# Ten modulation units summed on the tensor engine in four column groups, and one projection load issued earlier

## The chip, the cores and the metric

The kernel runs on one core of a Trainium2 chip. The metric is the device time of one execution in microseconds (us), the median of several. Matrix products run on the tensor engine (PE in the profile; PEld is its weight load, which overlaps), elementwise work on the vector engine (DVE) and the scalar engine (ACT); GpSimd (POOL) does little here, and the sync engine (SP) issues the DMA loads. Each engine works through its own queue in the order written there and waits at an instruction whose operands are not ready. Products accumulate in PSUM, in banks that hold 512 floats on each of 128 partitions.

## The reference

Two encoder layers over 256 tokens of width 1024: latent attention (MLA) and a dense feed-forward network (FFN) in layer 0, a Mamba-2 mixer and eight experts in layer 1. Each sublayer is modulated by shifts, scales and gates that come from a single conditioning row `c`:

```python
cond = jax.nn.silu(c)                                   # (1, 1024)
for i in range(DEPTH):
    mod = cond @ ada_w[i] + ada_b[i]                    # (1, 6144)
    sh1, sc1, g1, sh2, sc2, g2 = jnp.split(mod, 6, axis=-1)
    h = modulate(rmsnorm(x, norm_g[i, 0]), sh1, sc1)
    ...                                                 # y = mla_mixer(h, ...) or mamba2_mixer(h, ...)
    x = x + g1[:, None, :] * y
    h = modulate(rmsnorm(x, norm_g[i, 1]), sh2, sc2)
    ...                                                 # y = swiglu(h, ...) or moe_swiglu(h, ...)
    x = x + g2[:, None, :] * y
```

`cond @ ada_w[i]` is a product of one row with a 1024 x 6144 matrix, all float32: 4 MB of weights for every 1024 columns, and each weight is used once.

## The kernel before

The 6144 columns of a layer's `ada_w` are cut into 12 **units** of 512 columns. A unit is 1024 x 512 floats, loaded as two 1 MB tiles `raw` of 4 x 128 rows each (unit 2 as one of 4 and two of 2). Units 0 and 1 of layer 0 are the shifts `sh1` (channels 0 to 511 and 512 to 1023), 2 and 3 the scales `sc1`, 4 and 5 the gates `g1`, 6 and 7 `sh2`, 8 and 9 `sc2`. The result is wanted with channels on partitions, four columns of the tile `mod` for each unit.

A unit's product is made without the tensor engine's matrix work: row block k of the weights (128 rows) is multiplied by a scalar per partition, `cond[:, k]`, and added up over the eight blocks. This gives `acc`, 128 x 512, whose sum over partitions is still to be made. For units 4 to 9 that is one ACT instruction (`ada_sum`, L218) and seven on DVE (L220); for units 0 to 3, which stand at the start of the program, `ada_sums` makes two half sums per unit (L248 on ACT, L250 and L252 on DVE). Then matmuls with a column of ones (L229 in `ada_unit`, L263 in `ada_pair`), 128 columns of `acc` at a time, sum over partitions and put the result on partitions; a DVE addition of the bias (L231, L266) ends a unit. `ada_pair` also runs 34 matmuls on `ones` that nothing reads (`keep_warm`, L272).

The work around it, in the order of the program. `x` is loaded and transposed (L430). Units 0 and 2 give shift and scale of channels 0 to 511 (`make_gsc`, L280); `normmod` makes `tt` (L341, DVE) and `h` (L343, ACT) of these channels, blocks k = 0 to 3; the input projection, in plain float32, takes block after block (L448, six matmuls per block: `win_mm`), reading three loads of the projection's weights (`win`, blocks 0-2, 3-5 and 6-7). Units 1 and 3 do the same for blocks 4 to 7. Then come the norms of the latents (L303, L316, L317, L328), keys and values (L516, copied out by `v_sb` L548), and four rounds of queries (L516, L567, L573) and attention (scores `sc` L581 and L582, exponentials L588 and L590, transposes `tp` L597, outputs `o` L602 to L604); the rounds carry units 4 to 7, one each. The output projection (L358 to L360, on pairs of high and low parts) has two halves, which carry units 8 and 9. Its residual (L376) feeds the next norm (L303 to L328) and the FFN's first matmul (`gu`, L358).

A scheduler sets the order on each engine from the order of the code and its own costs, so rounds overlap: a unit's instructions are spread among those of the attention. SP's queue is the order of the loads. A tile `raw` is one of a pool of buffers; a load waits until its buffer's last reader is done.

The matmuls are float32 in two passes: one matmul leaves two records in the trace ("x96" are 48 matmuls).

Of the kernel before, what the change touches and what calls it, by code (L numbers as in the profile page):

```python
# [11 lines left out]
F32 = mybir.dt.float32  # L12
# [3 lines left out]
AF = mybir.ActivationFunctionType  # L16
ALU = mybir.AluOpType
AX = mybir.AxisListType
PSUM = bass.MemoryType.PSUM

P = 128
# [48 lines left out]
def rows(ap, n, off=0):  # L70

    return bass.AP(tensor=ap.tensor, offset=ap.offset + off, ap=[[P, n], [1, P]])
# [8 lines left out]
def body(ctx: ExitStack, tc, x, c, positions, ada_w, ada_b, norm_g,  # L81
# [5 lines left out]
    V, A, PE, G, SP = nc.vector, nc.scalar, nc.tensor, nc.gpsimd, nc.sync  # L87

    per = ctx.enter_context(tc.tile_pool(name="per", bufs=1, side="left"))
    rawp = ctx.enter_context(tc.tile_pool(name="rawp", bufs=8, side="left"))  # L90
    hlp = ctx.enter_context(tc.tile_pool(name="hlp", bufs=4, side="left"))
# [4 lines left out]
    nrm = dctx.enter_context(tc.tile_pool(name="nrm", bufs=2, side="right"))  # L96
# [11 lines left out]
    def pt(tag):  # L108
        pool, tag, n = banks[tag]
        return pool.tile([P, 512], F32, tag=tag, name=tag, bufs=n)  # L110
# [12 lines left out]
    def load(ap, k):  # L123

        n = ap.shape[1]
        t = raw(k * n).rearrange("p (k n) -> p k n", k=k)
        SP.dma_start(t, ap.rearrange("(k p) n -> p k n", p=P))
        return t
# [58 lines left out]
    cond = pd.tile([P, DC], F32, name="cond")  # L187
    A.activation(cond, cT, AF.Silu)
    ones = per.tile([P, P], F32, name="ones")
# [1 line left out]
    V.memset(ones, 1.0)  # L191
    eps_t = per.tile([P, 1], F32, name="eps_t")
    V.memset(eps_t, EPS)
    few = per.tile([P, 3], F32, name="few")
    warm, halfpi, zero = few[:, 0:1], few[:, 1:2], few[:, 2:3]
    V.memset(zero, 0.0)

    ej = per.tile([P, 2, S + 2 * NE], F32R, name="ej")
# [3 lines left out]
    ident = cst[:, C_ID:C_ID + P]  # L202
    vecs = pd.tile([P, 3, P], F32, name="vecs")

    vecT = pd.tile([P, 3, P], F32, name="vecT")
    mod = pd.tile([P, 2, 48], F32, name="mod")
# [6 lines left out]
    def ada_load(i, u):  # L213
        return load8(ada_w[i, :, u * 512:(u + 1) * 512])
# [7 lines left out]
    def ada_unit(i, u):  # L222

        acc = nrm.tile([P, 512], F32, tag="acc", name="acc")
        ada_sum(ada_load(i, u), acc)
        ps = pt("m")
        if i == 0 and u < 10:
            for m in range(4):
                PE.matmul(ps[:, m:m + 1], acc[:, m * P:(m + 1) * P], ones[:, 0:1], start=m == 0, stop=True,  # L229
                          skip_group_check=True)  # L230
            V.tensor_add(mod[:, i, 4 * u:4 * u + 4], ps[:, 0:4], vecT[:, 0, 48 * i + 4 * u:48 * i + 4 * u + 4])  # L231
        else:
            for m in range(4):
                PE.transpose(ps[:, m * P:(m + 1) * P], acc[:, m * P:(m + 1) * P], ident)
            dst = mod[:, i, 4 * u:4 * u + 4]
            for m in range(4):
                A.activation(acc[:, m * P:(m + 1) * P], ps[:, m * P:(m + 1) * P], AF.Copy,
                             accum_out=dst[:, m:m + 1])
            V.tensor_add(dst, dst, vecT[:, 0, 48 * i + 4 * u:48 * i + 4 * u + 4])

    def ada_sums(w):

        both = hlp.tile([P, 1024], F32, tag="wlo", name="acc2")
        acc = [both[:, z * 512:(z + 1) * 512] for z in range(2)]
        for k, wk in enumerate(t[:, k, :] for t in w for k in range(t.shape[1])):
            a = acc[k % 2]
            if k == 0:
                A.activation(a, wk, AF.Copy, scale=cond[:, k:k + 1])  # L248
            elif k == 1:
                V.tensor_scalar(a, wk, cond[:, k:k + 1], None, op0=ALU.mult)  # L250
            else:
                V.scalar_tensor_tensor(a, wk, cond[:, k:k + 1], a, op0=ALU.mult, op1=ALU.add)  # L252
        return acc

    def ada_pair(u, sums, warm=(0, 0)):

        ps = pt("m")
        for i, acc in enumerate(sums):
            keep_warm(warm[i])
            for z in range(2):  # L260
                for m in range(4):
                    c = 4 * i + m
                    PE.matmul(ps[:, c:c + 1], acc[z][:, m * P:(m + 1) * P], ones[:, 0:1],  # L263
                              start=z == 0 and c == 0, stop=z == 1, skip_group_check=True)
        four = lambda t: t.rearrange("p (i c) -> p i c", c=8)[:, :, 4 * u:4 * u + 4]
        V.tensor_add(four(mod[:, 0, 0:16]), ps[:, 0:8].rearrange("p (i c) -> p i c", c=4), four(vecT[:, 0, 0:16]))  # L266

    def keep_warm(n, bank="mm"):

        ps = pt(bank) if n else None  # L270
        for _ in range(n):
            PE.matmul(ps[:, :P], ones, ones, start=True, stop=True)  # L272

    gsc = pd.tile([P, 2, 2, DC], F32, name="gsc")

# [113 lines left out]
    with ExitStack() as lctx:  # L389
# [7 lines left out]
        def win_load(k0, n):  # L397
            return load(mla_w_in[0, k0 * P:(k0 + n) * P, :], n)


        SP.dma_start(cst[:, 0:C_V], consts[:, 0:C_V])
        x_in = load(x[0], 2)
        SP.dma_start(vecs[0:96, 0, :], rows(ada_b, 96))
        SP.dma_start(vecs[96:128, 0, :], rows(norm_g, 32))
        aw = {0: ada_load(0, 0)}
# [2 lines left out]
        SP.dma_start(vecs[0:3, 2, :], rows(mla_q_norm, 3))  # L408
        SP.dma_start(vecs[3:5, 2, :], rows(mla_kv_norm, 2))
        SP.dma_start(vecs[5:21, 2, :], rows(ssm_norm, 16))  # L410
        win = [win_load(0, 3)]
        aw[1] = ada_load(0, 1)
        aw[3] = ada_load(0, 3)
        pos_i = mi.tile([P, S], I32, tag="t2", name="pos_i", bufs=2)
        SP.dma_start(pos_i, bcast(positions, S))
        win += [win_load(3, 3), win_load(6, 2)]
        SP.dma_start(cst[:, C_V:], consts[:, C_V:C_KEY])


# [6 lines left out]
        for q in range(4):  # L426
            ps = pt("mm")
# [3 lines left out]
            A.copy(xT[:, 2 * q:2 * q + 2, :], ps.rearrange("p (a s) -> p a s", a=2))  # L431
        r = spread(pt("n"), r)
        vec_block(0, 128)
        sums = ada_sums(aw[0]), ada_sums(aw[2])
        ada_pair(0, sums, (8, 26))
        make_gsc(0, 0, 0, 4)
        normmod(0, 0, r, range(4), whole=h32)

# [10 lines left out]
                          skip_group_check=True)  # L449
        for k in range(4):  # L450
            win_mm(k, kv + rq + qq)
        sums = ada_sums(aw[1]), ada_sums(aw[3])
        ada_pair(1, sums)
        make_gsc(0, 0, 4, 8)
        normmod(0, 0, r, range(4, 8), whole=h32)

# [81 lines left out]
        wk = [packed(wkv[k][:, :, 0:64].unsqueeze(1)) for k in range(2)]  # L538
        for t in range(8):
            ps = pt("mm")  # L540
# [3 lines left out]
        for j in range(2):  # L544
            for nh in range(2):
                ps = pt("mm")
# [60 lines left out]
        for b in range(4):  # L607
            queries(b)
            attend(2 * b)
            attend(2 * b + 1)  # L610
            ada_unit(0, 4 + b)
        for half in range(2):
            w = load8(mla_w_out[0, :, half * 512:(half + 1) * 512])
            for m in range(2):
                ps = pt("mm")
                ws = unit8(w, m * 256, 256)
                for t in range(2):
                    mm3(ps[:, t * S:(t + 1) * S], list(zip(cols(ws, slice(t * P, (t + 1) * P)), at)))
                for t in range(2):
                    resid(ps[:, t * S:(t + 1) * S], 4 * half + 2 * m + t, 0, 0)  # L620
            ada_unit(0, 8 + half)
        make_gsc(0, 1)

    ph = scoped(dctx, "ph")
# [69 lines left out]
    with ExitStack() as lctx:  # L694
# [36 lines left out]
        ps, psb0 = pt("in"), pt("y")  # L731
# [9 lines left out]
        four = nrm.tile([P, 4, 2, SH], F32, tag="sq", name="four", bufs=2)  # L741
        xb, e, z, w = (four[:, i, :, :] for i in range(4))
        q = e
# [60 lines left out]
        m = decay_tiles()  # L804
# [808 lines left out]
```

## Time and profile before

| | |
|---|---|
| three runs | 1290.25, 1292.62, 1293.30 us (median 1292.62) |
| profiled execution | 1291.27 us, its span 1289.1 us |
| PE busy | 1244.1 us, 97% of the span |
| DVE busy | 857.4 us, 67% |
| ACT busy | 698.4 us, 54% |
| chain that ended last | PE 86%, DMA 4%, DVE 4%, ACT 3%, issue 2% |

The stage that the change touches, layer 0's attention with its modulation, is the first 162 us of the span; from the FFN on the program is as before. "Busy" counts a matmul until its modelled end, so PE at 97% is not PE at its peak: whether it streams or waits has to be read from the starts of its instructions. The chain of waits follows the last instruction back to what released it, piece by piece.

### The profile page before, as it was taken

What the parts mean: (1) busy time and instruction counts of PE and PEld (TensorE: products, weight loads), DVE (VectorE), ACT (ScalarE), POOL (GpSimd) and SP (SyncE); (2) the same over time, 40 slices, a digit from 0 to 9 for tenths busy, and PEclk for the clock granted to TensorE, in tenths of its full rate; (3) what the DMA queues carried; (4) which work ended last, traced back from release to release, by engine and by line L of the source; (5) the groups of instructions that cost most, each with busy time, mean ns of one, the idle gap of its engine ahead of it and who ended that gap; (6) DMA issues with size and microseconds to landing.
All of it is one profiled execution on the core that took longest, in us unless ns stands there. A gap on an engine that the chain in (4) does not pass through costs nothing.

```text
span 1289.1 us, 21161 instructions
## 1 busy us (share of the span) xinstructions
PE 1244.1 (97%) x8236; PEld 1006.7 (78%) x8236; DVE 857.4 (67%) x1314; ACT 698.4 (54%) x1162; POOL 18.3 (1%) x16
## 2 busy tenths in 40 slices
PE   7999999999999999998999999999999999999996
PEld 6768899999988999996648875488855688888652
DVE  7577787787789788853148870388902789988412
ACT  3468564455577767524157650477603676776312
POOL 4010000000000000000000000000000000000000
PEclk9999999999989999997999999999999999999999
DMA  9885569887933466425999999999999999998895
GB/s 343 313 299 188 196 239 349 325 308 272 321 124 127 164 213 213 164 99 203 421 422 419 421 394 409 421 421 420 395 382 420 420 421 398 387 352 312 329 421 214
DMA packets 104730, 407.96 MB, mean 316 GB/s; under 512 B 10401, under 2 KB 16046, under 8 KB 70958
## 3 DMA queue, kind: packets, MB, share of 16 engines
q1 hardware_dynamic: 104622, 406.53, 81.5%
q8 instruction: 66, 1.08, 0.3%
q14 instruction: 42, 0.34, 0.1%
HBM read 405.46 MB, written 1.05 MB: 315 GB/s over the span
## 4 chain that ended last, share of the span: by engine, by line
PE 86%; DMA 4%; DVE 4%; ACT 3%; issue 2%; SPq 0%; ACTq 0%; DVEq 0%
PE a L1291 18%; PE a L1383 12%; PE y L1336 10%; DMA raw<-in_moe_w_down_dram 4%; PE y L1402 3%; PE y L358 3%; PE gu L358 3%; PE gu L359 3%; PE gu L360 3%; PE y L359 3%; PE y L360 3%; PE in L360 2%; PE in L358 2%; PE in L359 2%; PE mm L448 2%
## 5 line engine op out<-in xcount | busy, mean ns | idle before, releaser
L159 DVE TENSOR_TENSOR wlo<-raw,whi 128x1024 fp32r<-128x1024 f32 x395 | 466.3, 1218 | 83.4 <-ACT whi L159 81.7
L159 ACT CAST whi<-raw 128x1024 fp32r<-128x1024 f32 x395 | 403.7, 1050 | 185.6 <-PE a L1291 41.6
L1383 PE MATMUL a<-raw,xe 128*64 128x384 f32 (+3 forms) x1280 | 161.6, 413 | 0.0
L1291 PE MATMUL a<-wlo,xe_hi 128*128 128x512 f32 (+1 forms) x464 | 153.2, 343 | 0.4
L1291 PE MATMUL a<-whi,xe_lo 128*128 128x512 f32 (+1 forms) x464 | 151.9, 339 | 0.0
L1383 PEld LDWEIGHTS a<-raw,xe 128*64 128x64 f32 x1280 | 92.0, 135 | 68.1 <-issue 51.7
L1304 DVE TENSOR_TENSOR sg<-sg,a 128x512 f32<-128x512 f32 (+2 forms) x36 | 22.0, 640 | 157.0 <-PE a L1383 145.1
L1291 PE MATMUL a<-whi,xe_hi 128*128 128x256 f32 (+1 forms) x464 | 111.2, 344 | 7.8 <-ACT whi L159 7.8
L220 DVE SCALAR_TENSOR_TENSOR acc<-raw,cond,acc 128x512 f32<-128x512 f32 x140 | 105.5, 766 | 5.8 <-ACT acc L218 4.3
L358 PE MATMUL gu<-hT_hi,whi 128*128 128x256 f32 x352 | 99.7, 284 | 1.2 <-ACT hT_hi L345 1.2
L1291 PEld LDWEIGHTS a<-wlo,xe_hi 128*128 128x128 f32 x464 | 87.0, 188 | 16.6 <-DVE wlo L159 4.2
L359 PE MATMUL gu<-hT_lo,whi 128*128 128x256 f32 x352 | 99.6, 283 | 0.0
L360 PE MATMUL gu<-hT_hi,wlo 128*128 128x256 f32 x352 | 99.1, 282 | 0.0
L1291 PEld LDWEIGHTS a<-whi,xe_lo 128*128 128x128 f32 x464 | 87.2, 188 | 9.7
L1291 PEld LDWEIGHTS a<-whi,xe_hi 128*128 128x128 f32 x464 | 75.9, 188 | 24.0 <-ACT whi L159 14.9
L1402 PE MATMUL y<-raw,at 128*64 128x512 f32 (+1 forms) x364 | 81.6, 586 | 0.9 <-DMA raw<-in_moe_w_down_dram 0.6
L358 PE MATMUL in<-hT_hi,whi 128*128 128x256 f32 (+1 forms) x264 | 75.9, 288 | 0.7 <-ACT whi L159 0.7
L360 PE MATMUL in<-hT_hi,wlo 128*128 128x256 f32 (+1 forms) x264 | 75.5, 287 | 0.5 <-DVE wlo L159 0.5
L359 PE MATMUL in<-hT_lo,whi 128*128 128x256 f32 (+1 forms) x264 | 74.7, 283 | 0.0
L358 PEld LDWEIGHTS gu<-hT_hi,whi 128*128 128x128 f32 x352 | 67.0, 191 | 1.5 <-ACT hT_hi L345 1.5
L360 PEld LDWEIGHTS gu<-hT_hi,wlo 128*128 128x128 f32 x352 | 67.0, 190 | 0.0
L359 PEld LDWEIGHTS gu<-hT_lo,whi 128*128 128x128 f32 x352 | 67.0, 190 | 0.0
(399 smaller groups left out, 2281.7 us busy)
## 6 DMA issues: line engine op xcount, KB each, us to landing
raw<-in_moe_w_gate_dram SPq DMA_DIRECT2D x88, 1024.0 KB, 7.1
raw<-in_moe_w_up_dram SPq DMA_DIRECT2D x88, 1024.0 KB, 12.8
raw<-in_moe_w_down_dram SPq DMA_DIRECT2D x85, 1024.0 KB, 15.9
raw<-in_ada_w_dram SPq DMA_DIRECT2D x47, 1024.0 KB, 8.0
raw<-in_ssm_w_in_dram SPq DMA_DIRECT2D x20, 1024.0 KB, 5.2
raw<-in_ffn_w_down_dram SPq DMA_DIRECT2D x11, 1024.0 KB, 8.4
raw<-in_ffn_w_gate_dram SPq DMA_DIRECT2D x10, 1024.0 KB, 8.4
raw<-in_ffn_w_up_dram SPq DMA_DIRECT2D x10, 1024.0 KB, 9.4
```

The lines of the kernel that those rows point to most:

```text
L159: return A.copy(hi, src), V.tensor_sub(lo, src, hi)
L220: V.scalar_tensor_tensor(acc, w[k // 4][:, k % 4, :], cond[:, k:k + 1], acc, op0=ALU.mult, op1=ALU.add)
L358: PE.matmul(ps, whi, ahi, start=(first and i == 0), stop=False, skip_group_check=skip)
L359: PE.matmul(ps, whi, alo, start=False, stop=False, skip_group_check=skip)
L360: PE.matmul(ps, wlo, ahi, start=False, stop=(last and i == n - 1), skip_group_check=skip)
L448: PE.matmul(ps, win[k // 3][:, k % 3, sl], h32[:, k, :], start=first and k == 0, stop=k == DC - 1, skip_group_check=True)
L1291: PE.matmul(bank[:, o:o + n], a[:, j, :], w[:, m], start=f, stop=l, skip_group_check=True)
L1304: V.tensor_mul(self.sg[:, sl], self.sg[:, sl], self.acc["u", b][:, :n])
L1336: PE.matmul(self.y[b], a, w[:, b * 512:(b + 1) * 512], start=f, stop=l, skip_group_check=True)
L1383: PE.matmul(bank[FEW * h:FEW * (h + 1), o // 2:(o + n) // 2], self.xhi[:, j, :], w[:, h, :], start=first, stop=last, skip_group_check=True)
L1402: res = PE.matmul(self.y[c0 // 512][FEW * h:FEW * (h + 1), c0 % 512:c0 % 512 + n], self.at[t][:, FEW * h:FEW * (h + 1)], ws[h], start=t == ...
```

## The change

Units 0 to 9 of layer 0 no longer go through DVE and ACT sums. `ada_rows` makes eight matmuls per unit: row block k of the weights is the moving operand (128 x 512), and the stationary operand is `cond[:, k]` repeated over 32 columns. Block k writes column group k mod 4, that is 32 of the bank's 128 partitions; blocks 4 to 7 accumulate onto blocks 0 to 3. DVE copies the bank to SBUF (`row`), and `ada_columns` makes four 128 x 1 matmuls per unit against `one4`, a column that is 1 on one partition of each group and 0 elsewhere: this adds up the four groups and puts the result on partitions. `keep_warm` is gone. Units 10 and 11 of layer 0 and all of layer 1 stay as they were.

The second load of the projection's weights (blocks 3 to 5) moves ahead of units 1 and 3, the third ahead of `pos_i`, and unit 3 is loaded in pieces of 4, 2 and 2 row blocks.

```diff
+    def ada_rows(w):
+
+
+        ps = pt("mm")
         for k, wk in enumerate(t[:, k, :] for t in w for k in range(t.shape[1])):
...
+            g = k % 4 * 32
+            PE.matmul(ps[g:g + 32, :], cond[:, k:k + 1].to_broadcast([P, 32]), wk, start=k < 4, stop=k >= 4,
+                      skip_group_check=True)
+        row = nrm.tile([P, 512], F32, tag="acc", name="row")
+        V.tensor_copy(row, ps)
+        return row
+
+    def ada_columns(units, rows):
 
         ps = pt("m")
...
+        for i, (u, row) in enumerate(zip(units, rows)):
+            for m in range(4):
+                PE.matmul(ps[:, 4 * i + m:4 * i + m + 1], row[:, m * P:(m + 1) * P], one4, start=i == m == 0,
+                          stop=True, skip_group_check=True)
+        for i, u in enumerate(units):
+            V.tensor_add(mod[:, 0, 4 * u:4 * u + 4], ps[:, 4 * i:4 * i + 4], vecT[:, 0, 4 * u:4 * u + 4])
...
+        V.reduce_sum(one4, ident.rearrange("p (g q) -> p g q", g=4)[:, :, 0], axis=AX.X)
...
-        win = [win_load(0, 3)]
+        win = [win_load(0, 3), win_load(3, 3)]
         aw[1] = ada_load(0, 1)
-        aw[3] = ada_load(0, 3)
+        u3 = ada_w[0, :, 1536:2048]
+        aw[3] = [load(u3[0:512, :], 4), load(u3[512:768, :], 2), load(u3[768:1024, :], 2)]
+        win += [win_load(6, 2)]
...
-        win += [win_load(3, 3), win_load(6, 2)]
...
-        sums = ada_sums(aw[0]), ada_sums(aw[2])
-        ada_pair(0, sums, (8, 26))
+        ada_columns((0, 2), [ada_rows(aw[u]) for u in (0, 2)])
...
-        sums = ada_sums(aw[1]), ada_sums(aw[3])
-        ada_pair(1, sums)
+        ada_columns((1, 3), [ada_rows(aw[u]) for u in (1, 3)])
...
-            ada_unit(0, 4 + b)
+            ada_columns((4 + b,), [ada_rows(ada_load(0, 4 + b))])
...
-            ada_unit(0, 8 + half)
+            ada_columns((8 + half,), [ada_rows(ada_load(0, 8 + half))])
```

In the changed kernel the new lines are L247 (the matmuls on the weights), L250 (the copy `row`), L258 (the column matmuls) and L261 (the addition); the lines behind them have numbers lower by 11 (L448 is L438 there, L358 is L347).

How the tensor engine's queue changes is shown at three places. First, the middle of the input projection: `mm` and `m` are PSUM tiles, `h32` the modulated input, a `raw` number is one loaded tile. Before, block 3 (raw_142, the second projection load) stood behind the column sums of units 1 and 3:

```order
L448 MATMUL mm_269<-h32_111,raw_130 128x256 x2
L263 MATMUL m_312<-ones_80,acc2_294 128x1 x8
L263 MATMUL m_312<-ones_80,acc2_303 128x1 x8
L448 MATMUL mm_267<-h32_111,raw_142 128x256 x2
L448 MATMUL mm_268<-h32_111,raw_142 128x256
```

The same place in the changed kernel (raw_133 is the second projection load, raw_135 to raw_143 are the pieces of units 1 and 3):

```order
L438 MATMUL mm_233<-h32_111,raw_133 128x256 x2
L247 MATMUL mm_258<-raw_135,cond_78 32x512 x4
L247 MATMUL mm_258<-raw_137,cond_78 32x512 x4
L247 MATMUL mm_269<-raw_139,cond_78 32x512 x4
L258 MATMUL m_280<-few_85,row_267 128x1 x4
L247 MATMUL mm_269<-raw_141,cond_78 32x512 x2
L247 MATMUL mm_269<-raw_143,cond_78 32x512 x2
L258 MATMUL m_280<-few_85,row_278 128x1 x4
L438 MATMUL mm_231<-h32_111,raw_133 128x256 x4
```

Block 3 now stands ahead of the units' matmuls, and nothing of the projection stands between these and block 4.

Second, the attention: unit 5's matmuls in the changed kernel (raw_770 and raw_772 are its two tiles; L591 to L593 are the attention's outputs, L570 and L571 its scores, L505 the next round's queries), with no counterpart before, where the tensor engine had only four column sums of unit 5:

```order
L247 MATMUL mm_774<-raw_770,cond_78 32x512
L591 MATMUL o_573<-pT_613,v_sb_416 64x128
L592 MATMUL o_573<-pT_613,v_sb_416 64x128
L593 MATMUL o_573<-pT_613,v_sb_416 64x128
L570 MATMUL sc_677<-kT_322,qT_321 128x128
L571 MATMUL sc_677<-kT_322,qT_321 128x256
L570 MATMUL sc_699<-kT_322,qT_321 128x128
L571 MATMUL sc_699<-kT_322,qT_321 128x256
L247 MATMUL mm_774<-raw_770,cond_78 32x512 x3
L247 MATMUL mm_774<-raw_772,cond_78 32x512 x4
L505 MATMUL mm_797<-lat0_399,wcp_793 128x256
```

The first of the eight stands alone, seven follow later. Unit 7's stand in three pieces (1, 4 and 3), unit 4's in two (5 and 3); units 6, 8 and 9 have their eight together.

Third, the end of the stage, before (L360 is the output projection, L303 the norm that follows):

```order
L359 MATMUL mm_1326<-aT_lo_529,whi_1331 128x256
L360 MATMUL mm_1326<-aT_hi_528,wlo_1332 128x256
L229 MATMUL m_1398<-ones_80,acc_1385 128x1 x4
L303 MATMUL m_1420<-ones_80,ss_1421 128x1 x2
L303 MATMUL m_1420<-ones_80,sq_1433 128x1 x2
```

and in the changed kernel:

```order
L348 MATMUL mm_1297<-aT_lo_490,whi_1302 128x256
L349 MATMUL mm_1297<-aT_hi_489,wlo_1303 128x256
L247 MATMUL mm_1360<-raw_1356,cond_78 32x512 x4
L247 MATMUL mm_1360<-raw_1358,cond_78 32x512 x4
L258 MATMUL m_1371<-few_85,row_1369 128x1 x4
L292 MATMUL m_1393<-ones_80,ss_1394 128x1 x2
L292 MATMUL m_1393<-ones_80,sq_1406 128x1 x2
```

Unit 9's matmuls, and its column sums that need the copy `row` of them, now stand between the last matmul of the output projection and the norm.

## Rows read from the trace of the kernel before

**Rows 1.** Windows: stretch and length, busy us (records) per engine, PE clock, DMA share, GB/s.

```profile
26.00:36.00 10.00, 10.00 (x35) 6.30 (x36) 9.85 (x16) 2.54 (x5) 0.00 (x0) 0.83 1.05 391
...
40.00:50.00 10.00, 10.00 (x40) 7.37 (x41) 5.26 (x17) 6.82 (x12) 0.00 (x0) 0.83 1.02 379
...
70.00:80.00 10.00, 8.96 (x37) 5.91 (x36) 6.20 (x11) 3.19 (x8) 0.00 (x0) 1.00 1.02 376
80.00:90.00 10.00, 8.96 (x40) 7.35 (x40) 7.10 (x17) 6.58 (x18) 0.00 (x0) 0.83 1.05 386
...
100.00:110.00 10.00, 9.76 (x64) 8.29 (x63) 8.63 (x28) 9.28 (x29) 0.00 (x0) 1.00 0.48 161
110.00:120.00 10.00, 10.00 (x67) 8.26 (x65) 7.40 (x23) 8.59 (x26) 0.00 (x0) 1.00 0.41 156
...
130.00:140.00 10.00, 8.41 (x60) 6.61 (x59) 8.91 (x21) 3.52 (x10) 0.00 (x0) 1.00 0.59 187
```

**Rows 2.** The chain of waits, first 60 us: start us, us, what.

```profile
19.00 0.81 DVE acc L252 x2
...
22.44 1.96 PE m L263 x16
...
24.43 0.17 DVE mod L266
...
25.95 10.57 PE mm L448 x36
36.53 3.47 PE m L263 x32
39.99 9.35 PE mm L448 x34
```

**Rows 3.** Timeline of ACT around 30 us: start, us, instruction, idle time before it.

```profile
30.40 0.72 ACT L248 ACTIVATE acc<-raw,cond 128x512 f32<-128x512 f32 x1 [2.43 <-DMA raw<-in_ada_w_dram]
```

**Rows 4.** Timeline of PE in the experts, near 643 us.

```profile
643.25 1.94 PE L1402 MATMUL y<-raw,at 128*64 128x512 f32 x8
645.12 0.39 PE L1200 MATMUL a<-psel,xt_lo 128*128 128x256 f32 x1
```

**Rows 5.** Groups of instructions by line, 60 to 157 us.

```profile
L220 DVE SCALAR_TENSOR_TENSOR acc<-raw,cond,acc 128x512 f32<-128x512 f32 x40 | 31.7, 810 | 0.4
L516 PE MATMUL mm<-lat,wcp 128*128 128x256 f32 x103 | 26.3, 403 | 0.8 <-DVE v_sb L548 0.8
...
L359 PE MATMUL mm<-aT_lo,whi 128*128 128x256 f32 x64 | 18.6, 293 | 0.0
...
L582 PE MATMUL sc<-kT,qT 98*128 98x256 f32 x32 | 9.7, 384 | 0.0
L597 PE MATMUL tp<-cst,pe 128*128 128x128 f32 x48 | 9.2, 278 | 0.0
...
L516 PE MATMUL mm<-raw,lat 128*128 128x512 f32 x16 | 7.0, 592 | 0.0
L602 PE MATMUL o<-pT,v_sb 128*64 128x128 f32 x32 | 6.9, 298 | 0.9 <-ACT pT L599 0.8
...
L581 PE MATMUL sc<-kT,qT 98*128 98x128 f32 x32 | 6.6, 288 | 1.0 <-ACT pe L590 1.0
...
L229 PE MATMUL m<-ones,acc 128*128 128x1 f32 x48 | 5.8, 242 | 0.3 <-DVE mod L231 0.3
...
L548 DVE COPY v_sb<-mm 128x512 f32<-128x512 f32 x4 | 2.7, 684 | 0.0
```

**Rows 6.** The chain of waits, 60 to 165 us.

```profile
97.12 0.36 PE o L602 x2
97.48 0.22 PE o L603 x2
...
114.45 0.43 PE mm L516 x2
...
122.17 0.12 PE mm L360
```

More of the change, by code (lines that the diff above doesn't have):

```diff
@@ L193, in body @@
     V.memset(eps_t, EPS)
-    few = per.tile([P, 3], F32, name="few")
-    warm, halfpi, zero = few[:, 0:1], few[:, 1:2], few[:, 2:3]
+    few = per.tile([P, 4], F32, name="few")
+    warm, halfpi, zero, one4 = (few[:, i:i + 1] for i in range(4))
     V.memset(zero, 0.0)
@@ L239, in ada_unit @@
             V.tensor_add(dst, dst, vecT[:, 0, 48 * i + 4 * u:48 * i + 4 * u + 4])
-    def ada_sums(w):
-        both = hlp.tile([P, 1024], F32, tag="wlo", name="acc2")
-        acc = [both[:, z * 512:(z + 1) * 512] for z in range(2)]
+    def ada_rows(w):
+        ps = pt("mm")
         for k, wk in enumerate(t[:, k, :] for t in w for k in range(t.shape[1])):
[L246 to L255, printed above, removed]
-        ps = pt("m")
[L258 to L272, printed above, removed]
+            g = k % 4 * 32
[5 more added lines that the diff above has]
+    def ada_columns(units, rows):
+        ps = pt("m")
+        for i, (u, row) in enumerate(zip(units, rows)):
[4 more added lines that the diff above has]
+            V.tensor_add(mod[:, 0, 4 * u:4 * u + 4], ps[:, 4 * i:4 * i + 4], vecT[:, 0, 4 * u:4 * u + 4])
     gsc = pd.tile([P, 2, 2, DC], F32, name="gsc")
```

## The prediction

> **What bounds the kernel now.** I read the windows first. In the attention stage the tensor engine is the busy one: from 60 to 157 us its windows are full but for four, which leave 1.04, 1.04, 0.24 and 1.59 us idle, 3.9 us together (one full window stands for the others) [rows 1]. [...] DVE is never full there, though it carries 40 sums of units 4 to 9, 31.7 us [rows 5].
>
> Busy is not streaming, so I counted the work from the steps between starts on the chain: 0.43 us for two records of 128x256, 0.22 for two of 128x128, 0.12 for one of L358 to L360 [rows 6]. Times the counts [rows 5] (L358 and L360 have as many records as L359, L603 and L604 as many as L602): queries and keys 103 x 0.215 = 22.1; output projection 192 x 0.12 = 23.0; values 7.0; scores 6.9 + 3.5; transposes 5.3; attention outputs 96 x 0.11 = 10.6; column sums about 5; norms and rotations about 2: 85 us of 97. The 12 us beside it are the 3.9 idle, the 1.7 of clock, up to 32 x 0.14 = 4.5 at the first of each output group (L602 0.36 against L603 0.22 [rows 6]), and 1.9 that I can't place. So whatever the sums on DVE hold up there is worth at most 12 us, and what is added to the tensor engine there is paid.
>
> The first 60 us are different. There the chain goes through the sums (19.00), the column sums (22.44), the addition (24.43) and the first projection matmuls (25.95), and again through the column sums at 36.53 to block 3 at 39.99 [rows 2]; the loads run at 391 GB/s without a pause, 1 MB in 2.7 us [rows 1].
>
> **The price of a unit on the tensor engine.** No row shows four groups at once. The nearest has two: four matmuls of 128x512, two in each group of 64 columns, start at 643.25 and let the next one start at 645.12, 1.87 us [rows 4]. One by one, at 7.0 us for 16 records [rows 5], they would take 3.5. So two groups run side by side in full: four rounds of 0.43, and 0.15 for the change of shape. With four groups side by side a unit's 16 records are four rounds, 1.72 + 0.15 = 1.87 us; with only two, 3.6; with none, 7.0. I take 1.87, since the row has all of its gain, and keep 3.6 for the range.
>
> [...]
>
> **First stage, units 0 to 3 and the moved load.** The sums of units 0 and 2 and `keep_warm` go. After 19.00 there remain two matmuls of unit 2's last piece (1.0), the copy `row` (0.68, as L548 [rows 5]), four column matmuls (8 records of 0.12, as 1.96 for 16 [rows 2]: 1.0), the same 1.52 from the addition to the first projection matmul (25.95 - 24.43), and hand-overs: 23.3 instead of 25.95, **-2.6**.
>
> Then 24 matmuls follow instead of 18, since block 3 is there early. 18 took 10.57 us for 7.7 us of work, because the clock was low in part (0.83 [rows 1, 2]). With the same loss of 2.9 they end at 23.3 + 10.3 + 2.9 = 36.5. The moved load puts units 1 and 3 back by 2.7 us: the first half of unit 3, waited for until 30.40 [rows 3], lands at 33.1 and its last piece near 35.8. That costs nothing, because these matmuls are behind block 3 in the queue anyway; without this cover it would be 2.7. From 36.5: units 1 and 3 and the first columns 4.9, the copy 0.7, columns 1.0, then 1.52 and hand-overs: block 4 starts at 44.8. Before, it starts at 39.99 plus six matmuls (2.6) plus the loss of a low clock (1.7, window 40 to 50): 44.3. So the first gain is given back: the columns and the modulation now stand between the last block of the first half and block 4, with nothing of the projection beside them, where before block 3 covered them. **+0.5**. From below: no clock lost ahead of block 4, -2.4. From above: that pause leaves the clock low for block 4, 1.7 more, +2.2.
>
> **Attention, units 4 to 9.** 40 sums on DVE and five on ACT go, six copies of 0.68 come. The column sums remain. Added are 48 matmuls on the weights. Units 6, 8 and 9 stand whole, 1.87 each. Pieces can't be packed: unit 4 in 5 and 3 costs 1.0 + 0.86 + 1.0, unit 5 in 1 and 7 costs 1.0 + 1.87, both 2.9; unit 7 in 1, 4 and 3 costs 3.0. **+14.4** of tensor work in a stretch that is full; 11.2 if the pieces stand in waits.
>
> Back come the waits that end with the sums. By name they are 0.8 on `v_sb` and 0.3 on the addition (sums ahead of both on DVE), 1.0 ahead of the first scores [rows 5], and with an engine that is never short of work the 1.7 of clock. The rest of the idle time is behind ACT's work on `aT` and `pT`, which remains but gets a freer queue. I take the idle time and clock in full, 5.6, and half of the unplaced 1.9: **-6.5**. Bounds: 3.8 and 12.
>
> **The end.** Unit 9's eight matmuls, the copy and the columns now stand between the output projection and the norm. Before, the sums were done by then. The copy is a wait that nothing behind it in the queue can fill: 0.68 and two hand-overs, **+0.9**; 0 if it hides behind the residual, 1.9 if it queues behind two residuals on DVE. The norm and the FFN are behind it, and from there the order is as before, so the delay is kept to the end.
>
> **Sum**: 0.5 + 14.4 - 6.5 + 0.9 = +9.3 on the profiled 1291.3 us gives 1300.6. The median of the runs lies 1.35 above that execution, 1301.9 by it; I say 1301.
>
> **Rivals.**
> 1. *Only two groups side by side.* 3.6 instead of 1.87 for a unit: about 9 more in the attention and 3.4 in the first stage, 1301 + 12 = 1313. For it: nothing shows four. Against: two cost nothing extra.
> 2. *The other side: the tensor engine waits more than its idle time says.* If all 12 us beside the counted work, the 4.5 at L602 too, are waits for `pT` and `pe` behind the sums on DVE and ACT, and the single pieces and the changes of shape stand in such waits (6 x 1.72 = 10.3): -2.4 + 10.3 - 12 + 0 = -4.1, 1287 on the profiled execution's scale and 1288.5 on the median's. It decides, for faster by more than 4 us, where the waits closed reach 11.9. For it: DVE at 8.9 of 10 in 130 to 140, the emptiest window of the tensor engine [rows 1]. Against: most windows are full.
> 3. *No change.* The early start is kept (-2.4), the pieces cost nothing (11.2), the waits return 7.5, the end costs 0.9: +2.2, 1294.
> 4. *The first stage's work doesn't count*, because loads set its end: then that term is 0, and the sum stays within a microsecond of mine; no case of its own.
>
> **Chances.** My forecast 0.42, between 1297 and 1306; two groups 0.15; no change 0.23; faster 0.2. About 0.3%, 4 us, is what a measurement tells from nothing. Faster by more 0.2, within 0.23, slower 0.57. The range for 8 in 10 runs from 1288, inside the second rival, to 1312, just short of the first.
>
> **What would show it.** In the changed profile: L247 of units 6, 8 and 9 at about 1.9 us for 16 records, with starts four at a time (3.6 and two at a time: first rival). The first projection matmul near 23.3, block 4 near 44.8. Full windows of the tensor engine from 60 on, a granted clock of 1.00 in 80 to 90, and DVE down by about 28 us; the FFN's first matmul about 9 us later than before. I am wrong if it comes no later, and then the term of the waits is the one that failed; if it comes on time with L247 as priced, there was more waiting among full windows than I counted.

## The result, and the profile after

The changed kernel takes 1305.76 us, the median of four runs (1302.77 to 1308.71), against 1292.59 of before in the same comparison: 1.0106 times, with a 95% interval of 1.0088 to 1.0124. It is slower by 13 us; the forecast was slower by 8, at 1301.

The page of the changed kernel's profile, its span and tensor engine, and the engines' shares of the chain that ended last:

```profile
span 1306.0 us, 21207 instructions
...
PE 1257.7 (96%) x8296; PEld 999.5 (77%) x8296; DVE 818.1 (63%) x1257; ACT 691.7 (53%) x1152; POOL 16.9 (1%) x16
...
PE 87%; DMA 4%; ACT 4%; DVE 3%; issue 1%; SPq 0%; DVEq 0%; ACTq 0%
```

The profiled execution took 1307.8 us, 2 more than the median, as that of before lies 1.3 below its own: the two traces differ by 16.9 us of span where the medians differ by 13. All of it has come up when the FFN begins: its first matmul starts at 179.24 instead of 162.15, 17.1 later. DVE has 39 us less to do (the forecast of 28 counted units 4 to 9 alone), and the kernel is slower all the same.

The windows that answer to [rows 1], of the changed kernel (stretch and length, busy us and records of PE, PEld, DVE, ACT, POOL, granted clock, DMA share, GB/s):

```profile
40.00:50.00 10.00, 7.51 (x41) 5.06 (x34) 6.32 (x19) 1.81 (x4) 0.00 (x0) 0.83 0.98 369
...
60.00:70.00 10.00, 10.00 (x48) 8.09 (x47) 3.54 (x9) 5.68 (x16) 3.92 (x4) 0.83 0.74 263
70.00:80.00 10.00, 10.00 (x32) 5.79 (x31) 2.77 (x4) 3.75 (x10) 0.00 (x0) 1.00 0.39 111
80.00:90.00 10.00, 9.32 (x46) 5.47 (x45) 3.21 (x8) 7.63 (x20) 0.00 (x0) 1.00 1.00 363
...
130.00:140.00 10.00, 10.00 (x73) 6.78 (x71) 6.09 (x19) 5.29 (x20) 0.00 (x0) 1.00 0.89 302
...
172.00:183.00 11.00, 9.27 (x45) 8.88 (x45) 4.77 (x14) 3.53 (x9) 0.00 (x0) 0.53 0.39 146
```

Most of the idle time has gone, as forecast: 70 to 80 and 130 to 140 are full where they had 1.04 us idle (waits for `v_sb` and an addition, both on DVE) and 1.59 (waits for `aT_hi` and `pT`, both from ACT). The low clock of 80 to 90 is gone, but 60 to 70 now has one, in a full window. New are also an idle quarter in 40 to 50, where before there was none, and a low clock for the whole end of the stage (0.53 in 172 to 183).

The chain of waits of the changed kernel in the first 50 us (start us, us, what):

```profile
21.74 0.24 DVE mod L261 x2
...
23.28 14.78 PE mm L438 x48
38.06 2.71 PE mm L247 x24
40.77 1.01 PE m L258 x8
...
42.87 0.70 DVE row L250
...
43.62 1.06 PE m L258 x8
...
46.31 9.84 PE mm L438 x36
```

Read against [rows 2]: the first projection matmul starts at 23.28, forecast 23.3. The 48 records of blocks 0 to 3 take 14.78 us for 10.3 of work. From 38 to 46 the chain goes through units 1 and 3, a copy, columns and the modulation, one after the other, and block 4 starts at 46.31, forecast 44.8 and 44.44 before.

The chain of the same kernel behind that, at the units and at the end of the stage:

```profile
100.35 0.98 PE mm L247 x2
...
116.69 1.85 PE mm L247 x16
...
129.66 0.97 PE mm L247 x2
...
131.72 0.99 PE mm L247 x8
...
134.22 0.99 PE mm L247 x6
...
167.56 0.42 DVE wlo L159
...
168.71 0.87 DVE xT L365 x2
169.58 1.13 DVE wlo L159
170.71 0.61 DVE row L250
...
171.37 1.05 PE m L258 x8
172.42 3.88 PE m L292 x20
...
179.24 0.80 PE gu L347 x2
```

A whole unit takes 1.85 us for 16 records (116.69), one matmul alone 0.97 or 0.98, a piece of 4 or 3 takes 0.99: the prices of the forecast to a few hundredths. So four column groups do run side by side: 16 records of 128x512 on all 128 columns took 7.0 us [rows 5], 16 in two groups 3.58 (the run with two groups). At the end unit 9's copy `row` stands on DVE behind a residual and behind a low part `wlo` of the FFN's first weights.

### The profile page after: what moved, and what is told of

Same layout as the page of the kernel before. It is cut to its first block, busy times and chain, and to the rows that moved or that the text cites. A ratio compares the mean times of both kernels' runs of the same rounds, so it can differ in the third digit from the quotient of the medians.

```text
span 1306.0 us, 21207 instructions
## 1 busy us (share of the span) xinstructions
PE 1257.7 (96%) x8296; PEld 999.5 (77%) x8296; DVE 818.1 (63%) x1257; ACT 691.7 (53%) x1152; POOL 16.9 (1%) x16
## 4 chain that ended last, share of the span: by engine, by line
PE 87%; DMA 4%; ACT 4%; DVE 3%; issue 1%; SPq 0%; DVEq 0%; ACTq 0%
PE a L1280 18%; PE a L1372 11%; PE y L1325 9%; PE y L1391 4%; PE y L347 3%; PE y L349 3%; PE y L348 3%; PE gu L347 3%; PE gu L348 3%; PE gu L349 3%; PE mm L505 2%; PE in L349 2%; PE in L347 2%; PE mm L438 2%; DMA raw<-in_moe_w_down_dram 2%; PE in L348 2%
## 5 line engine op out<-in xcount | busy, mean ns | idle before, releaser
L347 PE MATMUL gu<-hT_hi,whi 128*128 128x256 f32 x352 | 99.3, 283 | 1.2 <-ACT hT_hi L334 1.2
L349 PE MATMUL gu<-hT_hi,wlo 128*128 128x256 f32 x352 | 98.7, 280 | 0.0
L1280 PEld LDWEIGHTS a<-whi,xe_hi 128*128 128x128 f32 x464 | 76.0, 188 | 24.0 <-ACT whi L159 14.9
L347 PE MATMUL in<-hT_hi,whi 128*128 128x256 f32 (+1 forms) x264 | 76.0, 288 | 0.7 <-DVE r L303 0.7
L220 DVE SCALAR_TENSOR_TENSOR acc<-raw,cond,acc 128x512 f32<-128x512 f32 x98 | 72.3, 749 | 2.4 <-ACT acc L218 1.2
L347 PEld LDWEIGHTS gu<-hT_hi,whi 128*128 128x128 f32 x352 | 66.7, 190 | 1.5 <-ACT hT_hi L334 1.5
```

The source lines that it names most:

```text
L220: V.scalar_tensor_tensor(acc, w[k // 4][:, k % 4, :], cond[:, k:k + 1], acc, op0=ALU.mult, op1=ALU.add)
L347: PE.matmul(ps, whi, ahi, start=(first and i == 0), stop=False, skip_group_check=skip)
L349: PE.matmul(ps, wlo, ahi, start=False, stop=(last and i == n - 1), skip_group_check=skip)
L1280: PE.matmul(bank[:, o:o + n], a[:, j, :], w[:, m], start=f, stop=l, skip_group_check=True)
```

## The experiments

All of them are this kernel with the edit shown. The table gives the median, the ratio to the kernel before with its interval, and from each profile the start of the first projection matmul, of block 4, of the first transpose, of the output projection's last matmul, and of the FFN's first (us).

| kernel | median | ratio | first | block 4 | transposes | last out | FFN |
|---|---|---|---|---|---|---|---|
| before | 1292.6 | | 25.95 | 44.44 | 90.82 | 155.78 | 162.15 |
| changed | 1305.8 | 1.0106 [1.0088, 1.0124] | 23.28 | 46.31 | 92.43 | 167.64 | 179.24 |
| units 0-3 only | 1293.8 | 1.0028 [1.0008, 1.0049] | 23.42 | 46.18 | 93.81 | 160.13 | 166.14 |
| units 4-9 only | 1302.3 | 1.0086 [1.0065, 1.0106] | 25.76 | 45.28 | 88.03 | 163.22 | 175.24 |
| unit 9 on DVE | 1301.6 | 1.0086 [1.0066, 1.0105] | 23.23 | 44.96 | 90.90 | 166.11 | 173.72 |
| loads as before | 1303.0 | 1.0081 [1.0060, 1.0103] | 23.13 | 44.41 | 88.74 | 163.94 | 175.49 |
| two groups | 1324.1 | 1.0251 [1.0227, 1.0275] | 25.75 | 49.88 | 95.28 | 183.73 | 194.53 |
| units 8, 9 early | 1303.5 | 1.0097 [1.0074, 1.0120] | 23.38 | 46.22 | 92.27 | 169.82 | 177.08 |
| filler | 1306.8 | 1.0118 [1.0094, 1.0142] | 27.88 | 48.66 | 94.90 | 170.07 | 181.58 |
| units 0-3, loads as before, filler | 1293.6 | 1.0017 [1.0002, 1.0033] | 27.66 | 46.08 | 92.10 | 157.04 | 163.56 |
| units 0-3, loads as before | 1290.6 | 0.9992 [0.9976, 1.0009] | 23.08 | 44.61 | 89.64 | 154.79 | 160.96 |
| unit 4 only | 1298.0 | 1.0065 [1.0045, 1.0085] | 26.34 | 44.82 | 87.57 | 159.84 | 168.28 |
| units 0-4, loads as before | 1298.7 | 1.0058 [1.0038, 1.0079] | 23.17 | 43.17 | 87.50 | 159.76 | 167.70 |
| unit 4 only, early | 1294.7 | 1.0032 [1.0017, 1.0048] | 26.40 | 44.88 | 90.91 | 158.06 | 166.91 |

The medians of before in the shared comparisons were 1290.7 to 1292.0. The ratio and its interval are those of each comparison; the quotient of two medians can differ from it by a tenth of a per cent (units 0-3 only: 1.0014 by the medians). The intervals of "unit 9 on DVE", "loads as before" and "units 8, 9 early" overlap that of the changed kernel, so what these three bring is read from the starts in the table more than from the runs.

**Which part costs.** First the two halves of the change, each alone. Units 4 to 9 back on DVE:

```diff
-            ada_columns((4 + b,), [ada_rows(ada_load(0, 4 + b))])
+            ada_unit(0, 4 + b)
...
-            ada_columns((8 + half,), [ada_rows(ada_load(0, 8 + half))])
+            ada_unit(0, 8 + half)
```

> The changed kernel with units 4 to 9 summed on DVE again; units 0 to 3 and the loads stay as changed. Theory of the attention and the tail (the matmuls on the weights fill a tensor engine that was full from 90 us on, and unit 9's copy stands in the way of the norm): most of the 13 us goes, about 1296 remains, because block 4 of the projection still starts 2 us late and the clock is low twice behind it; the FFN's first matmul near 166. Rival, the first stage (its delay is carried through and is most of the loss, the attention's matmuls stand in waits): 1302 to 1305.

And the kernel before with only these two lines changed the other way (and the new helpers added):

> The kernel before with only units 4 to 9 moved to the tensor engine; units 0 to 3, the matmuls that nothing reads and the loads as before. Theory of the attention and the tail: 1301 to 1304, nearly all of the loss; 16 records of a unit take 1.85 us as in the changed kernel, and the last 12 us up to the FFN look as there. Rival, the first stage: within 3 us of before, 1290 to 1296.

1293.8 and 1302.3. The two delays at the FFN, 4.0 and 13.1 us, add up to the whole 17.1; by the ratios, 0.28% and 0.86% against 1.06%, whose intervals allow the same. The attention and the end are three quarters of the loss; that the first stage carried most of it is out.

**Is added tensor work paid?** Two groups of 64 columns instead of four of 32, the same matmuls:

```diff
-            g = k % 4 * 32
-            PE.matmul(ps[g:g + 32, :], cond[:, k:k + 1].to_broadcast([P, 32]), wk, start=k < 4, stop=k >= 4,
+            g = k % 2 * 64
+            PE.matmul(ps[g:g + 64, :], cond[:, k:k + 1].to_broadcast([P, 64]), wk, start=k < 2, stop=k >= 6,
...
-        V.reduce_sum(one4, ident.rearrange("p (g q) -> p g q", g=4)[:, :, 0], axis=AX.X)
+        V.reduce_sum(one4, ident.rearrange("p (g q) -> p g q", g=2)[:, :, 0], axis=AX.X)
```

> The changed kernel with two column groups of 64 instead of four of 32, the same matmuls in the same order, so only the price of a unit changes. Theory (the tensor engine is full from 90 us on, so its added work is paid): a unit of 16 records takes 3.6 us instead of 1.85, and with units 5 to 9 in the full stretch and the end the time rises by 8 to 12 us over the changed kernel, to 1314 to 1318. Rival (the matmuls on the weights stand in waits and the loss is elsewhere): up to 3 us more, 1306 to 1309.

1324.1, 18 us above the changed kernel and more than either side expected (its profile is 15.3 behind at the FFN): I had counted only units 5 to 9, and block 4 already starts 3.6 us later. The groups of this kernel by line, 60 to 190 us, and one whole unit on its chain:

```profile
L247 PE MATMUL mm<-raw,cond 128*64 128x512 f32 x96 | 26.6, 603 | 0.0
```

```profile
168.06 3.58 PE mm L247 x16
```

The changed kernel has 14.9 us in the group's place. Of the difference of 11.7, unit 9 has 1.7; the other 10.0 stand between the last input projection matmul and the output projection's end, and there this kernel needs 119.8 us (63.93 to 183.73) instead of 107.0 (60.65 to 167.64). What is added in the attention is paid, here with a surcharge of 2.8 that I can't place.

**The end of the stage.** From the output projection's last matmul to the FFN's first the changed kernel needs 11.6 us, the one before 6.4. Unit 9 alone back on DVE:

```diff
+            if half == 0:
+                ada_columns((8,), [ada_rows(ada_load(0, 8))])
+            else:
+                ada_unit(0, 9)
```

> The changed kernel with unit 9 alone summed on DVE again. In the changed kernel 11.4 us pass from the output projection's last matmul to the FFN's first, before 6.1. Theory: 1.9 us of unit 9's matmuls, 1.7 of waiting for its copy behind a weight's low part on DVE and the longer norm go, 4 to 5 us, so 1301. Rival (the sum on DVE comes late there and the tail waits as long, or the delay is one of the clock alone): within 2 us of the changed kernel, 1304 to 1307.

1301.6, 4 us less, and 7.6 us in that place instead of 11.6. Then everything kept on the tensor engine, but the matmuls and copies of units 8 and 9 written ahead of their half of the output projection:

```diff
             w = load8(mla_w_out[0, :, half * 512:(half + 1) * 512])
+            late = [ada_rows(ada_load(0, 8 + half))]
...
-            ada_columns((8 + half,), [ada_rows(ada_load(0, 8 + half))])
+            ada_columns((8 + half,), late)
```

> The changed kernel with the matmuls and the copy of units 8 and 9 written ahead of their half of the output projection instead of behind it; the column sums stay behind. Nothing is left out, the tensor engine's work is the same. Theory (behind the last half it is the wait for the copy and the stopped engine that cost, beside 1.9 us of matmuls that are paid either way): 2 to 4 us less than the changed kernel, 1302 to 1304. Rival (the tail costs only the matmuls): no difference, 1305 to 1307.

1303.5, 2 us less, and 2.2 at the FFN. Its timeline at the end of the stage shows the column sums right behind the projection, without the wait of 1.6 us:

```profile
169.82 0.28 PE L349 MATMUL mm<-aT_hi,wlo 128*128 128x256 f32 x1
169.93 0.95 PE L258 MATMUL m<-few,row 128*128 128x1 f32 x8
170.74 0.58 PE L292 MATMUL m<-ones,ss 128*128 128x1 f32 x4
```

The place needs 7.3 us; the output projection ends 2.2 later, for the matmuls that are now in front. So the end cost about 5 us: 1.9 of matmuls, and 3 of a copy behind DVE's queue and of the norm behind it.

**The moved load.** The loads in the order of before (and unit 3 in two pieces again), units on the tensor engine:

```diff
-        win = [win_load(0, 3), win_load(3, 3)]
+        win = [win_load(0, 3)]
         aw[1] = ada_load(0, 1)
...
+        aw[3] = ada_load(0, 3)
...
+        win += [win_load(3, 3), win_load(6, 2)]
```

> The changed kernel with the loads in the order of before: second and third projection load behind units 1 and 3, unit 3 in two pieces. Then units 1 and 3 land 2.7 us earlier, their matmuls stand ahead of block 3 in the tensor engine's queue, and block 3 covers columns, copy and modulation. Theory (the moved load takes that cover away): block 4 starts near 39 instead of 46.3, and 5 to 7 us go, 1299 to 1301. Rival (the second projection load then ends the stage, or the gain is lost to the clock): within 2 us of the changed kernel.

1303.0, 3 us less where 5 to 7 were expected. The timeline of its tensor engine, 22 to 47 us:

```profile
23.13 11.85 PE L437 MATMUL mm<-h,raw 128*128 128x256 f32 x36 [1.41 <-ACT h L332]
34.91 2.78 PE L247 MATMUL mm<-raw,cond 128*32 128x512 f32 x24
37.65 1.05 PE L258 MATMUL m<-few,row 128*128 128x1 f32 x8
38.63 1.06 PE L247 MATMUL mm<-raw,cond 128*32 128x512 f32 x8
40.51 1.05 PE L258 MATMUL m<-few,row 128*128 128x1 f32 x8 [0.81 <-DVE row L250]
41.42 5.74 PE L437 MATMUL mm<-h,raw 128*128 128x256 f32 x24
```

Block 3, now behind the columns, covers the modulation: block 4 follows it without a break (24 records from 41.42 on). I had put it at 39, without adding up that the units' matmuls, two sets of columns and a wait for the copy stand ahead of block 3 one after the other (6.5 us). The same order with units 4 to 9 on DVE:

> Units 0 to 3 on the tensor engine with the loads in the order of before and no filler; units 4 to 9 on DVE as before. Theory (the moved load cost the cover; the filler of the run with it cost the early start, 27.7 instead of 23.1): block 4 at 44.4 as in the run with the loads alone, so no gain and no loss, 1290 to 1293, and 1 to 3 us less than with the moved load. Rival (the first stage's remaining loss is the clock alone): as with the moved load, 1293 to 1295.

1290.6, a ratio of 0.9992: the first stage on the tensor engine costs nothing when the load isn't moved, and with it 0.28%. At the FFN the two profiles are 5.2 us apart, about 1 of it by a lower clock ahead of block 4 (0.66 against 0.83 in 20 to 30). The start of 23.1 instead of 25.95 is used up by what stands ahead of block 3. The moved load is the first stage's loss.

**The removed filler.** Matmuls that nothing reads, back in the waits of units 0 and 2:

```diff
         for i, (u, row) in enumerate(zip(units, rows)):
+            keep_warm(warm[i])
...
+        keep_warm(warm[2])
...
-        ada_columns((0, 2), [ada_rows(aw[u]) for u in (0, 2)])
+        ada_columns((0, 2), [ada_rows(aw[u]) for u in (0, 2)], (6, 8, 8))
```

> The changed kernel with 22 matmuls that nothing reads put back into the waits of the first stage, 6 and 8 around unit 2's matmuls and 8 behind the columns. Theory (the removed filler kept the clock up there): the low clock ahead of block 0 to 3 is 3.4 us long as before instead of 6.8, the first projection matmul stays at 23.3, block 4 starts 1.7 us earlier and 1 to 3 us go, 1303 to 1305. Rival (the filler doesn't decide the clock, or delays unit 2): within 1 us of the changed kernel or slower.

No gain, 1306.8. Its timeline, 23 to 28 us:

```profile
23.06 2.05 PE L269 MATMUL mm<-ones 128*128 128x128 f32 x16
24.95 0.95 PE L259 MATMUL m<-few,row 128*128 128x1 f32 x8
25.76 2.03 PE L269 MATMUL mm<-ones 128*128 128x128 f32 x16
```

The filler (L269) is longer than the waits that it was to fill: the first projection matmul starts at 27.88 instead of 23.28. The granted clock is 0.57 in 18 to 22 and 1.00 in 22 to 45, where the changed kernel has 0.66 in 20 to 30; what that gave was lost to the 4.6 us. With the loads of before and units 4 to 9 on DVE:

> Units 0 to 3 on the tensor engine, the loads in the order of before, the filler of the run before this, and units 4 to 9 on DVE as before. Theory (the early start of 2.6 us is kept when block 3 covers the columns and the clock isn't lower): first scores about 3 us earlier than before, 1288 to 1290. Rival (the first stage's gain runs into DVE's sums of units 4 and 5 and is lost there): no change, 1291 to 1293.

1293.6, no gain either, for the same reason (27.66); without the filler the same kernel is the one at 1290.6.

**A unit where the tensor engine waits.** In the run with units 4 to 9 the transposes start 2.8 us earlier than before, with unit 4's matmuls already done. So unit 4 alone, on the kernel before:

```diff
-            ada_unit(0, 4 + b)
+            if b == 0:
+                ada_columns((4,), [ada_rows(ada_load(0, 4))])
+            else:
+                ada_unit(0, 4 + b)
```

> The kernel before with unit 4 alone on the tensor engine. In the run with units 4 to 9 there the first transposes came 2.8 us earlier than before although unit 4's 2.9 us of matmuls stood ahead of them. Theory (what is added where the tensor engine waits costs nothing, what is added behind it is paid in full): the early start is kept to the end, 2 to 3 us less than before, 1288 to 1290. Rival (the early start needs unit 5's sums gone from DVE as well, or is lost in the attention's waits): within 1.5 us of before.

1298.0, slower by 7 where faster by 2 or 3 was expected. The transposes do start 3.3 us earlier, but from there to the end of the output projection it needs 72.3 us, 65.0 before. Two groups of the tensor engine by line in that stretch, queries and column sums, first before (91.15 to 156 us), then here (87.9 to 160):

```profile
L516 PE MATMUL mm<-lat,wcp 128*128 128x256 f32 x36 | 9.2, 388 | 0.0
L229 PE MATMUL m<-ones,acc 128*128 128x1 f32 x26 | 3.1, 237 | 0.0
```

```profile
L539 PE MATMUL mm<-lat,wcp 128*128 128x256 f32 x42 | 11.5, 391 | 0.0
L229 PE MATMUL m<-ones,acc 128*128 128x1 f32 x32 | 3.9, 242 | 0.0
```

So the earlier start is no gain: six records of queries, six of scores and eight of unit 5's column sums (two of the 26 above start just ahead of the first transpose), 3.3 us by the steps of the forecast, stand behind the first transpose now and stood ahead of it before. From the last input projection matmul to the end of the output projection, which counts all of them on both sides, this kernel needs 102.4 us instead of 98.7, for 2.9 of added matmuls. Its windows:

```profile
60.00:70.00 10.00, 10.00 (x43) 7.71 (x43) 2.54 (x6) 7.22 (x19) 3.92 (x4) 1.00 0.44 162
70.00:80.00 10.00, 9.32 (x38) 5.50 (x37) 2.93 (x6) 3.02 (x7) 0.00 (x0) 1.00 0.91 314
...
100.00:110.00 10.00, 8.74 (x52) 6.32 (x51) 8.75 (x27) 7.50 (x25) 0.00 (x0) 1.00 0.62 211
...
130.00:140.00 10.00, 8.64 (x63) 6.99 (x61) 8.95 (x23) 5.24 (x17) 0.00 (x0) 1.00 0.13 31
```

DVE is busy for 5.5 of the 20 us from 60 to 80 (before: 15.96), and the tensor engine idles for 4.0 us in 100 to 140 (before: 1.8); 1.8 us of that are waits of transposes for `pe` from DVE, of which before had none. With the first stage too:

> The run before this (units 0 to 3 on the tensor engine, loads as before, no filler) with unit 4 on the tensor engine too. Theory: both gains, as far as there are any, add up: 1287 to 1290. Rival: the same as before, 1291 to 1293.

1298.7, the same, and the same 72.3 us. To see whether the displaced sums do it, unit 4's matmuls were written ahead of the first queries:

```diff
+        row4 = ada_rows(ada_load(0, 4))
         for b in range(4):
             queries(b)
...
-                ada_columns((4,), [ada_rows(ada_load(0, 4))])
+                ada_columns((4,), [row4])
```

> The run with unit 4 alone on the tensor engine, with unit 4's matmuls and copy written ahead of the first queries instead of behind the first round of attention. In that run (1298.0) unit 4's matmuls read their two tiles as late as 79 to 84 us, unit 5's loads and its sums on DVE came later than before, DVE stood nearly empty from 60 to 80 us and was full in the attention. Here the eight matmuls stand together behind the values, and unit 5's sums right behind the values' copies in DVE's queue. Theory (the late reading of the tiles pushed the other units' sums into the full stretch): 5 to 9 us less than that run, 1288 to 1292. Rival (any unit on the tensor engine ahead of the scores costs what it adds, or the sums' place on DVE doesn't matter): 1294 to 1298.

1294.7, inside the range of the rival; the theory asked for 1292 at most. Unit 5's sums are back in 70 to 80 (windows of this run):

```profile
70.00:80.00 10.00, 10.00 (x45) 5.45 (x44) 5.72 (x9) 1.79 (x6) 0.00 (x0) 1.00 0.89 310
...
130.00:140.00 10.00, 7.22 (x47) 5.06 (x45) 7.40 (x21) 4.30 (x14) 0.00 (x0) 1.00 0.44 131
```

and the stretch needs 67.1 us, but the transposes start at 90.91, as before, and the queries, scores and column sums stand ahead of them as before. From the last input projection matmul to the end of the output projection it is 100.5 us, 1.8 better than behind the first round; unit 4's matmuls, whole instead of in two pieces, are 1.0 of that, which leaves 0.8 for the displaced sums and all else in the profiles (that of unit 4 behind the first round is of an execution 3.3 us below its median). The waits for `pe` have gone, but 2.8 us are idle in 130 to 140. What else holds up unit 4's two versions, and the end there, is open. No version here is shown to beat the kernel before.

## Why the prediction was right, and where its terms were off

**What bounds the kernel** was read rightly: the attention has no free tensor engine. Units 4 to 8, priced at 12.5 without unit 9, lengthen the way from the last input projection matmul to the last of the output projection by 6.6 us with units 4 to 9 alone (57.92 to 163.22, before 57.08 to 155.78) and by 8.3 in the changed kernel (60.65 to 167.64). So 4 to 6 us came back; the term was -6.5. The tensor engine's idle time on this way fell by 2.9 us in both (3.9 before, 1.0 after), and 1.3 are in no window's idle time. The 1.7 between the two runs is the low clock. The forecast's 1.7 is 0.17 of the 10 us of 80 to 90 at 0.83 [rows 1]; in steps of 2 us the trace of before has a granted clock of 0.90, 0.50 and 0.75 from 80 to 86 and 1.00 from 86 to 90. At 0.50 the projection's records came at half the rate in that trace (5 in 28 to 30, 10 in 32 to 34 at 1.00). That an engine never short of work gets this back was the author's estimate, and the runs don't agree on it: the run with units 4 to 9 alone has 1.00 in 60 to 70 and in 80 to 90, but the changed kernel has 0.83 in 60 to 70, a full window, in place of 80 to 90.

**The price of a unit**, 1.87, was 1.85, with pieces at 0.97 to 0.99. The first rival, two groups, fell; its kernel has the 3.6 us for a unit that the forecast gave it (3.58 at 168.06), and shows that this would have cost 18 us, not 12.

**The first stage** is the first term that was mis-sized, +0.5 with an upper bound of 2.2. With units 0 to 3 alone it measured +4.0 at the FFN in the profile and 0.28% in the runs; in the changed kernel the last input projection matmul starts 3.6 us later (60.65, before 57.08). The start at 23.3 came as worked out, and the cover that the moved load takes away was named. In this profile blocks 0 to 3 lost 4.5 us (14.78 for 10.3) instead of 2.9, at a granted clock of 0.66 in 20 to 30, before 0.85. That part comes and goes between executions and is not the change's: the run with unit 9 on DVE has the same first stage, a clock of 0.83 there, and this timeline of the tensor engine:

```profile
23.23 13.48 PE L438 MATMUL mm<-h,raw 128*128 128x256 f32 x48 [1.41 <-ACT h L332]
...
44.96 9.67 PE L438 MATMUL mm<-h,raw 128*128 128x256 f32 x36 [1.65 <-ACT h L332]
```

Block 4 at 44.96 is the forecast's 44.8. What stays in that run too is the low clock when block 4 starts (0.83 in 40 to 50), behind the idle time ahead of it, which the forecast had only as its bound: its last input projection matmul starts at 59.12, 2.0 later than before. This is the step that was set too low.

**The end** is the second: 1.9 of matmuls and 0.9, where 5.2 were measured. The step "the copy is a wait that nothing fills" was right; its price went by two hand-overs, and its bound by two residuals on DVE. In the trace the copy stands behind `wlo`, the low part of the FFN's next weights, which is in DVE's queue ahead of it. And the norm that follows takes 3.88 us on the chain, before 2.5 in three pieces:

```profile
156.85 0.91 PE m L303 x8
...
157.83 0.43 ACT sq L289
...
158.30 1.07 PE m L303 x8
```

The clock is low from the norm on (0.53 in 172 to 183); before, the norm ran at a granted clock of 1.00 (156 to 160), and it was low behind it (0.51 in 160 to 167). That the wait for the copy brought the low clock is not shown: with unit 9 written ahead of the projection that wait is gone, and 172 to 183 has 0.53 as well. Written so, the same work costs 2 us less.

**The second rival**, that all 12 us beside the counted work were waits, fell too: with DVE relieved of all these sums, 4 to 6 came back, as said above. Where they came back can't be read from the first transpose, since in both kernels 3.3 us of queries, scores and column sums moved behind it, as with unit 4 alone.

**In sum**, by the changed kernel's profile: 3.6 to the last input projection matmul, 8.3 from there to the end of the output projection, 5.2 from there to the FFN, together 17.1. The forecast had 0.5, 6.0 and 2.8. Of the first, about 1.3 is the longer low clock of this one execution ahead of block 4. All three were too small, and none made up for another; the median of 1305.8 lies just inside the 1297 to 1306 of the forecast, and 17.1 us by the profile would not. So the mechanism was right, and that the number came this near is in part luck. That the medians differ by 13 and not by 17 has no term of its own: the runs of the changed kernel spread over 6 us, and its profiled one is among the slower.

Open: what decides the clock ahead of the projection. The removed filler alone does not: of four profiles with the first stage of before, filler included, three have 0.85 to 0.87 in 20 to 30 and one 0.72 (units 4 to 9 alone); of seven with four column groups and no filler, three have 0.83 and four 0.66.

## What to carry to other kernels

Work that goes from an engine with time to spare to the one that bounds the stage is paid for, even when packing makes it nearly four times cheaper (1.85 us for 16 records instead of 7.0): here 12.5 us of matmuls cost 6.6 to 8.3, and what the other engine got free was worth the 4 to 6 between them. Before an earlier start is called a gain, count what moved behind it (with unit 4 alone the transposes start 3.3 us earlier, and 3.3 us of other work stands behind them). A load that moves ahead is worth its place only if what it feeds doesn't lose its use as cover: block 3, done early, left the column sums bare (block 4 at 46.31, before 44.44). And at a stage's end, look for what stands in the helper engine's queue ahead of a new copy, here the next stage's weights (1.13 us of `wlo`).

## What the hardware showed that I had not expected

The same instructions met different clocks: 0.66 and 0.83 in 20 to 30 in two profiles with the same first stage (the changed kernel and the one with unit 9 on DVE), which is 1.3 us up to block 4. In the changed kernel a low clock came with three waits of the tensor engine that a chain of small steps made (ahead of block 0, 0.66 in 20 to 30; of block 4, 0.83 in 40 to 50; of the norm, 0.53 in 172 to 183), but also once in a full window (0.83 in 60 to 70). And one kernel's profiled execution can lie 7 us above its median (units 0-3 with the loads as before: 1297.96 against 1290.6, clock 0.974), so a single execution does not order kernels that are half a per cent apart.
